# A depthwise convolution of 31 taps: for three of four channel chunks GpSimd sums eight of the taps

## The chip, the cores and the metric

The kernel runs on one core of a Trainium2 chip. The core's engines work side by side, each through its own queue in program order, and wait for each other at semaphores: TensorE (PE, matmuls; PEld its weight loads), VectorE (DVE), ScalarE (ACT), GpSimd (POOL), and SyncE (SP), which issues the DMAs. The metric is the time of one execution on the device in microseconds, less is better. Everything is in float32; a matmul in full precision is made of three passes over a high and a low part of its operands.

## What is computed

One decoder layer of 1024 tokens and 1024 channels. The part that the change touches is the causal convolution of group B: 512 channels, each with its own 31 taps along the sequence.

```python
def _conformer_conv(u, conv_w, conv_b, norm_g, norm_b):
    a, g = jnp.split(u, 2, axis=-1)
    glu = a * jax.nn.sigmoid(g)
    y = lax.conv_general_dilated(
        glu, conv_w[:, None, :], window_strides=(1,),
        padding=[(CONV_K - 1, 0)],
        feature_group_count=CONV_CH) + conv_b
    y = _layernorm(y, norm_g, norm_b)
    return jax.nn.silu(y)
...
proj = h @ w_in                       # q, k, v, index q/k/w, conv input
attn_out = _dsa_attention(q, k, v, qi, ki, wi)   # top 256 keys of a row
conv_out = _conformer_conv(cu, conv_w[i], conv_b[i], ...)
x = x + gt1 * (concat([attn_out, conv_out]) @ w_out)
u = square(relu(h2 @ w_up));  x = x + gt2 * (u @ w_down);  rmsnorm
```

## The kernel before, in words

The sequence is worked in two halves of 512 tokens (hf 0 and 1), with blocks of 128 tokens for attention (0 to 3 and 4 to 7). Each engine's queue has a fixed order. A scheduler makes it from the steps of the strings ORDER and TAIL and from a table of priorities PR, where a lower number is more urgent; the work of a step with a high number fills the gaps that the scheduler sees in its own estimate. The numbers that matter: loading weights ("feed") 32050; the convolution of the first half ("conv0") 998450 and of the second ("conv1") 401000; the projections to q 400000; the search passes 150050 and up; conv_norm and conv_out 190500 and 998500; the MLP 1000000.

Weights come in units (load_unit, from line 161): SP issues the DMA into one of two wraw buffers of two units each, ScalarE copies the unit to its high part whi (line 184), and GpSimd subtracts it from the unit to give the low part wlo (line 185), 128 x 512 numbers. The high and the low parts stand in a ring of WB = 3 tiles of two units, six units, so a unit's whi waits until TensorE has finished with the unit six before it. The projections to q and to the indexer's q run in mm3_pair (line 128, matmuls at line 137): for pairs of token blocks, over the 8 slices of the contraction, the passes high-high, high-low, low-high, so that every third matmul reads wlo. A q projection of half the blocks uses eight units: four for two pairs of blocks each, and then four others. Ahead of it stands the g projection (conv input and gate, 16 units, matmuls at line 126), which ends in glu.

The convolution (conv_chunk, line 634) works on a chunk j of 128 channels on the partitions and 512 tokens. A chunk's sum is built in the one PSUM tile cv. VectorE's tensor_scalar (line 641) makes tap 0 and adds the bias, then 30 scalar_tensor_tensor (line 643) multiply a shifted view of glu (SBUF) by the tap's weight cwT and add cv; the last writes y, in SBUF. With four chunks in each half these are 8 and 240 instructions. y of the first half uses the buffer "y0" that the sums of the modulation (adacc) used before; these are read last by the matmuls of line 537. conv_norm (BN at line 864, line 871) normalises over channels after a transpose on TensorE, conv_out (line 873) transposes back and applies SiLU on ScalarE.

Around it stand the searches for the 256th score of each row (line 660): for each of 31 bits ScalarE's Sign pass counts (line 680), and VectorE sets a flag and the next trial value (lines 682, 683), for two blocks in turn. A search thus has 62 flags. select (from line 686) makes the mask, attention and attention1 use it. The search "s3" (blocks 2 and 3) runs beside the first q projection, "s7" (blocks 6 and 7) beside the last convolution chunks, "s5" follows. out_proj(1) comes after the last attention; the first 11 groups of the first half's MLP (line 964 on) fill TensorE's gaps and must be done before it, since their weights come ahead of out_proj's in the ring.

Of the kernel before, what the change touches and what calls it, by code (L numbers as in the profile page):

```python
# [15 lines left out]
OP = mybir.AluOpType  # L16
# [10 lines left out]
CK = 31  # L27
# [17 lines left out]
RV = True  # L45
ORDER = "Q0 g0 i2 c q0 i3 s3 Q1 m S3 q1 a0 g1 a1 n0 a2 z0 a3 i6 i7 o i5 h i4 s7 s5"
WB = 3
FLAGP = False
START = "x0 x1 x2 x3 a0 p0 x4 x5 x6 x7 a1 p1 a2 p2 a3"
WORK = "a0 t0 t1 t2 t3 e0 h0 a1 e1 k0 h1 a2 e2 k1 r4 t4 t5 h2 a3 e3 k2 h3 k3 t6 t7"  # L50
# [22 lines left out]
def layer(ctx, tc, x, c, positions, w_ada, b_ada, g_mix, w_in, conv_w, conv_b,  # L73
          conv_norm_g, conv_norm_b, w_out, g_mlp, w_up, w_down, g_final, out, dump=None):
    nc = tc.nc
    V, A, P, T, SP = nc.vector, nc.scalar, nc.gpsimd, nc.tensor, nc.sync
# [4 lines left out]
    @contextmanager  # L81
    def prio(p):
        old = tc.cur_priority
        tc.cur_priority = p
        yield
        tc.cur_priority = old
# [17 lines left out]
    def cv_tile(n=512):  # L104
        return psum.tile([128, n], FT, name="cv", bufs=1)
# [33 lines left out]
    def split_w(raw, n, lo_engine=None):  # L139
        hi = wpool.tile([128, 1024], FR, name="whi", bufs=WB)  # L140
        lo = wpool.tile([128, 1024], FR, name="wlo", bufs=WB)
        with prio(PR["feed"]):
            A.activation(hi[:, :n], raw[:, :n], AF.Copy)
            (lo_engine or P).tensor_tensor(lo[:, :n], raw[:, :n], hi[:, :n].bitcast(FT), op=OP.subtract)
        return hi, lo
# [15 lines left out]
    def load_unit(src, nch, cols, gate=None, dst=None):  # L161
        if not ring:
            ring["raw"] = [wpool.tile([128, 1024], FT, name="wraw", bufs=2) for _ in range(2)]
            ring["hi"] = [wpool.tile([128, 1024], FR, name="whi", bufs=WB) for _ in range(WB)]
            ring["lo"] = [wpool.tile([128, 1024], FR, name="wlo", bufs=WB) for _ in range(WB)]
            ring["n"] = ring["m"] = 0
# [27 lines left out]
    cwT = const.tile([128, 4, CK], FT, name="cwT")  # L194
# [410 lines left out]
    ych, glus = {}, {}  # L605
# [28 lines left out]
    def conv_chunk(j, hf):  # L634
        tc.cur_priority = PR["conv1" if hf else "conv0"]
        if j == 0:
            ych[hf] = (ea if hf else ey).tile([128, 4, 512], FT, name="y", tag="ga" if hf else "y0", bufs=1)
        y = ych[hf][:, j, :]
        gl = glus[hf][:, j, :]
        s = cv_tile()  # L640
        V.tensor_scalar(s, gl[:, 0:512], cwT[:, j, 0:1], convb[:, j:j + 1], op0=OP.mult, op1=OP.add)
        for tap in range(1, CK):
            V.scalar_tensor_tensor(y if tap == CK - 1 else s, gl[:, tap:tap + 512], cwT[:, j, tap:tap + 1], s,  # L643
                                   op0=OP.mult, op1=OP.add)


    twice = const.tile([128, 64], FT, name="twice")
# [449 lines left out]
    for j in range(4):  # L1097
        conv_chunk(j, 1)
# [166 lines left out]
```

## Time and profile before

| | |
|---|---|
| median of 3 runs | 1375.25 us (1374.19 to 1385.54) |
| profiled execution | 1377.54 us, span 1375.8 us |
| TensorE busy | 1268.3 us, 92% |
| VectorE busy | 974.8 us, 71% |
| ScalarE busy | 683.5 us, 50% |
| GpSimd busy | 482.0 us, 35%, 396 instructions |

The span runs from the first to the last recorded instruction; the profiled execution's own time is 1.7 us longer. The chain is the sequence of work, each piece released by the one ahead of it, that ended last; only what shortens or lengthens it moves the time. "xN" counts instructions, "idle before, releaser" is how long the engine waited ahead of an instruction and for whom.

### The profile page before, as it was taken

What the parts mean: (1) busy time and instruction counts of PE and PEld (TensorE: products, weight loads), DVE (VectorE), ACT (ScalarE), POOL (GpSimd) and SP (SyncE); (2) the same over time, 40 slices, a digit from 0 to 9 for tenths busy, and PEclk for the clock granted to TensorE, in tenths of its full rate; (3) what the DMA queues carried; (4) which work ended last, traced back from release to release, by engine and by line L of the source; (5) the groups of instructions that cost most, each with busy time, mean ns of one, the idle gap of its engine ahead of it and who ended that gap; (6) DMA issues with size and microseconds to landing.
All of it is one profiled execution on the core that took longest, in us unless ns stands there. A gap on an engine that the chain in (4) does not pass through costs nothing.

```text
span 1375.8 us, 19421 instructions
## 1 busy us (share of the span) xinstructions
PE 1268.3 (92%) x6686; PEld 1065.7 (77%) x6686; DVE 974.8 (71%) x2074; ACT 683.5 (50%) x1376; POOL 482.0 (35%) x396
## 2 busy tenths in 40 slices
PE   4677899989998899989999999899999999999997
PEld 4676789978887678767887879777878877888875
DVE  4879889999898899997878762473443386343457
ACT  3323358855764888768983552333122223333332
POOL 1333434422144234452223216422222244444453
PEclk9688999999999899999999999999999999999999
DMA  9337735522143123222111122352111134323332
GB/s 319 121 115 224 226 79 155 139 62 70 31 139 110 60 70 93 92 70 61 62 47 54 62 77 85 130 192 83 47 45 49 54 107 162 93 91 101 94 98 91
DMA packets 135690, 139.55 MB, mean 101 GB/s; under 512 B 8877, under 2 KB 109833, under 8 KB 135592
## 3 DMA queue, kind: packets, MB, share of 16 engines
q1 hardware_dynamic: 135424, 138.22, 32.2%
q8 instruction: 52, 0.85, 0.3%
q14 instruction: 46, 0.38, 0.1%
q10 hardware_dynamic: 168, 0.11, 0.0%
HBM read 126.23 MB, written 12.06 MB: 101 GB/s over the span
## 4 chain that ended last, share of the span: by engine, by line
PE 68%; DVE 21%; DMA 4%; issue 3%; ACT 3%; POOL 1%; ACTq 0%; POOLq 0%; DVEq 0%; SPq 0%
PE mm L126 25%; PE mc L126 13%; PE mm L137 9%; PE tp L126 7%; DMA wa<-in_w_ada_dram 3%; PE po L841 2%; PE tp L834 2%; DVE acc L521 2%; DVE cv L643 1%; PE tp L309 1%; PE po L748 1%; PE mc L592 1%; DVE acc L1018 1%; PE mc L822 1%; DVE acc L316 1%
## 5 line engine op out<-in xcount | busy, mean ns | idle before, releaser
L185 POOL TENSOR_TENSOR wlo<-wraw,whi 128x512 fp32r<-128x512 f32 x310 | 416.7, 1352 | 754.2 <-ACT whi L184 698.0
L184 ACT ACTIVATE whi<-wraw 128x512 fp32r<-128x512 f32 x310 | 193.9, 629 | 292.1 <-PE mm L126 143.1
L126 PE MATMUL mm<-half,whi 128*128 128x512 f32 x608 | 207.4, 407 | 0.6 <-ACT half L957 0.6
L680 ACT ACTIVATE sj<-score,bits 128x512 uint8<-128x512 f32 (+5 forms) x186 | 163.2, 877 | 23.0 <-DVE bits L683 11.0
L643 DVE SCALAR_TENSOR_TENSOR cv<-glu,cwT,cv 128x512 f32<-128x512 f32 x232 | 174.0, 750 | 0.8
L126 PE MATMUL mm<-whi,uh 128*128 128x512 f32 x344 | 141.7, 412 | 14.3 <-DVE sq L979 8.2
L126 PE MATMUL mc<-half,whi 128*128 128x512 f32 x416 | 149.0, 390 | 0.1
L126 PE MATMUL mm<-whi,ul 128*128 128x512 f32 x344 | 138.8, 404 | 3.0 <-DVE ul L986 3.0
L126 PE MATMUL mm<-wlo,uh 128*128 128x512 f32 x344 | 139.4, 405 | 0.0
L984 DVE TENSOR_TENSOR sq<-sq 128x512 f32<-128x512 f32 x42 | 46.0, 1096 | 126.1 <-ACT sq L983 126.1
L1018 DVE TENSOR_TENSOR acc<-mm,acc 128x512 f32<-128x512 f32 x152 | 104.3, 687 | 39.8 <-PE mm L126 38.9
L126 PE MATMUL mc<-half,wlo 128*128 128x512 f32 x336 | 131.1, 390 | 0.0
L126 PEld LDWEIGHTS mm<-half,whi 128*128 128x128 f32 x608 | 114.2, 192 | 20.0 <-ACT half L957 0.8
L137 PE MATMUL mm<-whi,half 128*128 128x256 f32 x640 | 121.8, 286 | 3.2 <-DVE wi L450 3.0
L126 PE MATMUL mm<-half,wlo 128*128 128x512 f32 x304 | 123.1, 405 | 0.0
L137 PEld LDWEIGHTS mm<-whi,half 128*128 128x128 f32 x640 | 102.9, 194 | 5.7 <-issue 3.1
L126 PE MATMUL mc<-h,whi 128*128 128x512 f32 x256 | 99.9, 390 | 0.0
L126 PEld LDWEIGHTS mm<-whi,uh 128*128 128x128 f32 x344 | 66.5, 193 | 37.0 <-DVE sq L979 10.8
L137 PE MATMUL mm<-wlo,half 128*128 128x256 f32 x320 | 91.2, 285 | 0.0
L126 PEld LDWEIGHTS mc<-half,whi 128*128 128x128 f32 x416 | 78.0, 188 | 16.6 <-ACT half L957 0.5
L126 PEld LDWEIGHTS mm<-whi,ul 128*128 128x128 f32 x344 | 66.6, 194 | 18.7 <-DVE ul L986 4.3
L126 PEld LDWEIGHTS mm<-wlo,uh 128*128 128x128 f32 x344 | 66.8, 194 | 13.2
(312 smaller groups left out, 2657.4 us busy)
## 6 DMA issues: line engine op xcount, KB each, us to landing
wraw<-in_w_up_dram SPq DMA_DIRECT2D x108, 256.0 KB, 2.8
wraw<-in_w_down_dram SPq DMA_DIRECT2D x108, 256.0 KB, 2.8
wa<-in_w_ada_dram SPq DMA_DIRECT2D x48, 512.0 KB, 4.5
wraw<-in_w_in_dram SPq DMA_DIRECT2D x33, 256.0 KB, 2.8
wraw<-in_w_in_dram SPq DMA_DIRECT2D x64, 128.0 KB, 2.9
wraw<-in_w_out_dram SPq DMA_DIRECT2D x32, 256.0 KB, 2.7
xs<-in_x_dram SPq DMA_DIRECT2D x8, 512.0 KB, 4.5
x<-in_x_dram SPq DMA_DIRECT2D x8, 512.0 KB, 4.3
```

What stands on the lines that cost most here:

```text
L126: T.matmul(ps, x, y, start=first and i == 0, stop=last and i == 3 * n - 1)
L137: T.matmul(ps[:, i * 256:(i + 1) * 256], rows[i][k][x], w[k][y], start=m == 0, stop=m == len(steps) - 1)
L184: A.activation(hi, raw, AF.Copy)
L185: P.tensor_tensor(lo, raw, hi.bitcast(FT), op=OP.subtract)
L309: T.matmul(t[:, j, :], xs[b][:, k * 128:(k + 1) * 128], dg[b], start=True, stop=True)
L521: V.scalar_tensor_tensor(accs[s], w, cond[:, k:k + 1], accs[s], op0=OP.mult, op1=OP.add)
L643: V.scalar_tensor_tensor(y if tap == CK - 1 else s, gl[:, tap:tap + 512], cwT[:, j, tap:tap + 1], s, op0=OP.mult, op1=OP.add)
L680: A.activation(sj[:, :L], score[b], AF.Sign, bias=bits[:, col].bitcast(FT), accum_out=cnt[:, col])
L834: T.transpose(t[:, 2 * i + u, :], sbp[u][:, (i0 + i) * 128:(i0 + i + 1) * 128], ident)
L841: T.matmul(po[:, hp % 2], vhl[:, i0 + i, g].rearrange("p a d -> p (a d)"), p[:, 2 * i:2 * i + 2, :], start=i0 + i + j == 0, stop=i0 + i == ...
L984: V.tensor_tensor(sq, sq, sq, op=OP.mult)
L1018: V.tensor_tensor(acc[b][:, cols], ps, acc[b][:, cols], op=OP.add)
```

## The change

A new constant CP = 8. For the chunks 0, 1 and 2 of each half (chunk 3 stays as it was) GpSimd makes the taps 23 to 30: eight tensor_scalar, the first into y, the others into the place of the next chunk's y as scratch, and after each of those a tensor_tensor that adds the scratch to y. VectorE makes taps 0 to 22 in cv as before, and then adds cv and y to y with one tensor_tensor. In all GpSimd gets 48 multiplications and 42 additions, VectorE loses 48 scalar_tensor_tensor and gets 6 tensor_tensor.

```diff
+CP = 8
...
         y = ych[hf][:, j, :]
         gl = glus[hf][:, j, :]
+
+
+        nv = CK - CP if j < 3 else CK
+        for tap in range(nv, CK):
+            pr = y if tap == nv else ych[hf][:, j + 1, :]
+            P.tensor_scalar(pr, gl[:, tap:tap + 512], cwT[:, j, tap:tap + 1], None, op0=OP.mult)
+            if tap > nv:
+                P.tensor_tensor(y, pr, y, op=OP.add)
         s = cv_tile()
         V.tensor_scalar(s, gl[:, 0:512], cwT[:, j, 0:1], convb[:, j:j + 1], op0=OP.mult, op1=OP.add)
-        for tap in range(1, CK):
+        for tap in range(1, nv):
             V.scalar_tensor_tensor(y if tap == CK - 1 else s, gl[:, tap:tap + 512], cwT[:, j, tap:tap + 1], s,
                                    op0=OP.mult, op1=OP.add)
+        if nv < CK:
+            V.tensor_tensor(y, s, y, op=OP.add)
```

In the changed kernel all line numbers behind this function are 11 higher, those ahead of it 1 higher.

GpSimd's queue before, in the last part of the g projection ("x3" are three instructions that read alike; row 26 ends with the last unit but one of the g projection, row 28 is its last unit and the first two of the q projection, row 31 its units 3 to 6, and row 33 begins with units 7 and 8; score is the causal mask of a block, glu the copy of the taps' overlap):

```order
24 L185 TENSOR_TENSOR wlo<-wraw,whi 128x512 x6
25 L620 COPY glu<-glu 128x30
26 L185 TENSOR_TENSOR wlo<-wraw,whi 128x512 x3
27 L601 AFFINE_SELECT score_595<-score_595 128x128
28 L185 TENSOR_TENSOR wlo<-wraw,whi 128x512 x3
29 L620 COPY glu<-glu 128x30
30 L601 AFFINE_SELECT score_594<-score_594 128x128
31 L185 TENSOR_TENSOR wlo<-wraw,whi 128x512 x4
32 L620 COPY glu<-glu 128x30
33 L185 TENSOR_TENSOR wlo<-wraw,whi 128x512 x35
```

After, the same place. Line 186 is line 185 of before; lines 646 and 648 are the new multiplication and addition. Rows 28 and 33 are the last two units of the g projection; row 45, the next subtraction, is the first unit of the q projection.

```order
26 L186 TENSOR_TENSOR wlo<-wraw,whi 128x512 x2
27 L646 TENSOR_SCALAR y<-glu,cwT 128x512 x2
28 L186 TENSOR_TENSOR wlo<-wraw,whi 128x512
29 L602 AFFINE_SELECT score_595<-score_595 128x128
30 L646 TENSOR_SCALAR y<-glu,cwT 128x512
31 L648 TENSOR_TENSOR y<-y 128x512
32 L646 TENSOR_SCALAR y<-glu,cwT 128x512
33 L186 TENSOR_TENSOR wlo<-wraw,whi 128x512
34 L648 TENSOR_TENSOR y<-y 128x512
35 L646 TENSOR_SCALAR y<-glu,cwT 128x512
36 L648 TENSOR_TENSOR y<-y 128x512
```

Where subtractions and small operations stood alone, the first multiplications now stand ahead of the g projection's last two units. Further on in the same queue, from the sixth unit of the q projection (row 73) to its seventh and eighth, which are the first two of row 82:

```order
73 L186 TENSOR_TENSOR wlo<-wraw,whi 128x512
74 L648 TENSOR_TENSOR y<-y 128x512
75 L621 COPY glu<-glu 128x30
76 L646 TENSOR_SCALAR y<-glu,cwT 128x512
77 L648 TENSOR_TENSOR y<-y 128x512
78 L646 TENSOR_SCALAR y<-glu,cwT 128x512
79 L648 TENSOR_TENSOR y<-y 128x512
80 L646 TENSOR_SCALAR y<-glu,cwT 128x512
81 L648 TENSOR_TENSOR y<-y 128x512
82 L186 TENSOR_TENSOR wlo<-wraw,whi 128x512 x28
```

Of the first half's 24 multiplications and 21 additions 16 stand ahead of the q projection's first unit (row 45), 27 ahead of its third (row 59) and all 45 ahead of its seventh (row 82), where before there was nothing but other subtractions and four small operations; then 28 units follow without any of them. The second half's 45 stand in rows 83 to 128, 15 for each chunk, with runs of four units between the chunks and single ones inside the second and third.

VectorE's queue at the last tap of the second half, before (line 696 begins the selection after the search s7; line 775 prepares v for the last attention group):

```order
1027 L643 SCALAR_TENSOR_TENSOR y<-glu,cwT,cv 128x512
1028 L682 TENSOR_SCALAR flag<-cnt 128x1
1029 L683 TENSOR_SCALAR bits<-bits,flag 128x1
1030 L864 BN_STATS st_5235<-tp 128x6
1031 L865 BN_AGGR mv<-st_5235 128x2
1032 L682 TENSOR_SCALAR flag<-cnt 128x1
1033 L864 BN_STATS st_5235<-tp 128x6
1034 L979 TENSOR_SCALAR sq<-mm 128x512
1035 L683 TENSOR_SCALAR bits<-bits,flag 128x1
1036 L775 TENSOR_TENSOR vhl<-vv,vhl 128x16x64
1037 L682 TENSOR_SCALAR flag<-cnt 128x1
1038 L696 TENSOR_SCALAR thrs<-bits 128x1
```

And after, where line 652 is 643, 693 and 694 are 682 and 683, 875 is 864, and 1029 is 1018 (the MLP's sum):

```order
863 L652 SCALAR_TENSOR_TENSOR y<-glu,cwT,cv 128x512
864 L990 TENSOR_SCALAR sq<-mm 128x512
865 L694 TENSOR_SCALAR bits<-bits,flag 128x1
866 L693 TENSOR_SCALAR flag<-cnt 128x1
867 L875 BN_STATS st_5283<-tp 128x6
868 L1029 TENSOR_TENSOR acc<-mm,acc 128x512
869 L992 TENSOR_TENSOR sq<-sq 128x512
870 L1029 TENSOR_TENSOR acc<-mm,acc 128x512
871 L997 TENSOR_TENSOR ul<-sq,uh 128x512
872 L1029 TENSOR_TENSOR acc<-mm,acc 128x512
873 L694 TENSOR_SCALAR bits<-bits,flag 128x1
```

The last tap, which stood right ahead of the selection, now has 35 flags of the search between it and the selection (row 988), and the normalisation's rows lie among these. At the earlier steps (first flag of s3, its selection, the first attention, the end of the fourth) VectorE has the same number of convolution instructions behind it as before, within one or two, up to the middle of s7. TensorE's order is the same as before up to the middle of the second half's g projection. At the end of the last attention 72 matmuls of the first half's MLP are still to come in the order before, and 142 after.

## Rows read from the trace of the kernel before

**Rows 1.** The page: busy time by engine, and the chain that ended last.

```profile
PE 1268.3 (92%) x6686; PEld 1065.7 (77%) x6686; DVE 974.8 (71%) x2074; ACT 683.5 (50%) x1376; POOL 482.0 (35%) x396
...
PE 68%; DVE 21%; DMA 4%; issue 3%; ACT 3%; POOL 1%; ACTq 0%; POOLq 0%; DVEq 0%; SPq 0%
PE mm L126 25%; PE mc L126 13%; PE mm L137 9%; PE tp L126 7%; DMA wa<-in_w_ada_dram 3%; PE po L841 2%; PE tp L834 2%; DVE acc L521 2%; DVE cv L643 1%; PE tp L309 1%; PE po L748 1%; PE mc L592 1%; DVE acc L1018 1%; PE mc L822 1%; DVE acc L316 1%
```

**Rows 2.** Windows of 25 us: length, busy time (count) by engine, clock, DMA.

```profile
200.00:225.00 25.00, 25.00 (x210) 24.96 (x210) 24.15 (x70) 21.47 (x57) 11.64 (x11) 1.00 0.45 127
250.00:275.00 25.00, 25.00 (x187) 24.00 (x187) 24.14 (x79) 19.18 (x52) 11.29 (x9) 1.00 0.53 139
275.00:300.00 25.00, 21.13 (x117) 17.48 (x116) 23.73 (x62) 12.85 (x39) 7.46 (x6) 0.93 0.28 74
525.00:550.00 25.00, 25.00 (x113) 20.67 (x112) 24.13 (x59) 21.68 (x39) 11.61 (x9) 1.00 0.33 99
625.00:650.00 25.00, 25.00 (x132) 20.30 (x131) 17.60 (x50) 23.73 (x44) 7.27 (x6) 1.00 0.21 64
```

**Rows 3.** The chain of waits in order of time: start, us, piece.

```profile
175.28 1.50 PE po L537 x8
189.06 11.15 PE mm L126 x49
200.20 56.17 PE mm L137 x468
```

**Rows 4.** Timeline of GpSimd, 178 to 209 us: start, us, instruction, [idle before].

```profile
178.78 0.29 POOL L601 TENSOR_SCALAR_AFFINE_SELECT score<-score 128x128 f32<-128x128 f32 x1
...
187.52 1.30 POOL L185 TENSOR_TENSOR wlo<-wraw,whi 128x512 fp32r<-128x512 f32 x1 [4.73 <-ACT whi L184]
...
193.98 1.29 POOL L185 TENSOR_TENSOR wlo<-wraw,whi 128x512 fp32r<-128x512 f32 x1 [2.62 <-ACT whi L184]
195.69 1.29 POOL L185 TENSOR_TENSOR wlo<-wraw,whi 128x512 fp32r<-128x512 f32 x1 [0.41 <-ACT whi L184]
199.42 2.66 POOL L185 TENSOR_TENSOR wlo<-wraw,whi 128x512 fp32r<-128x512 f32 x2 [2.44 <-ACT whi L184]
...
208.27 4.10 POOL L185 TENSOR_TENSOR wlo<-wraw,whi 128x512 fp32r<-128x512 f32 x3 [6.04 <-ACT whi L184]
```

**Rows 5.** Single lines on VectorE: count, shortest/median/longest ns, first and last start.

```profile
L643 DVE SCALAR_TENSOR_TENSOR cv<-glu,cwT,cv x232: 705/750/757, 162.1 to 569.0; 128x512 f32<-128x512 f32 x116
L643 DVE SCALAR_TENSOR_TENSOR y<-glu,cwT,cv x8: 739/745/749, 209.3 to 569.8; 128x512 f32<-128x512 f32 x8
...
L521 DVE SCALAR_TENSOR_TENSOR acc<-wa,cond,acc x42: 734/747/1851, 91.1 to 172.3; 128x512 f32<-128x512 f32 x42
...
L683 DVE TENSOR_SCALAR bits<-bits,flag x186: 173/208/216, 196.3 to 724.0; 128x1 int32<-128x1 int32 x186
```

**Rows 6.** Groups by line and form: count, busy us, mean ns, idle before.

```profile
L1018 DVE TENSOR_TENSOR acc<-mm,acc 128x512 f32<-128x512 f32 x152 | 104.3, 687 | 39.8 <-PE mm L126 38.9
...
L495 DVE TENSOR_TENSOR qs<-qn,qs 128x512 fp32r<-128x512 f32 x14 | 13.2, 942 | 1.7 <-ACT qs L494 1.5
...
L601 POOL TENSOR_SCALAR_AFFINE_SELECT score<-score 128x128 f32<-128x128 f32 x6 | 1.9, 322 | 3.2 <-DVE score L599 3.2
...
L192 POOL MEMSET ones<- 128x128 f32 x1 | 0.2, 204 | 0.3 <-POOLq L1254 0.3
...
L1254 POOL MEMSET const-float32-0.0<- 128x1 f32 x1 | 0.1, 98 | 0.2 <-issue 0.2
```

**Rows 7.** Timeline of ScalarE, 207 to 220 us.

```profile
208.87 0.63 ACT L184 ACTIVATE whi<-wraw 128x512 fp32r<-128x512 f32 x1
...
219.00 0.63 ACT L184 ACTIVATE whi<-wraw 128x512 fp32r<-128x512 f32 x1 [0.24 <-issue]
```

**Rows 8.** Windows of line 643 alone: VectorE busy (count), clock, DMA.

```profile
525.00:550.00 25.00, 12.76 (x17) 1.00 0.33 99
550.00:575.00 25.00, 9.73 (x13) 1.00 0.32 96
```

## The prediction

> **What bounds the kernel now.** I read the page's busy line first, because it says which engine can't be the place to save. TensorE is busy in 92% of the span, VectorE in 71%, GpSimd in 35%, and the chain of work that ended last gives TensorE 68%, VectorE 21% and GpSimd 1%; the conv taps of line 643 hold 1% of it [rows 1]. So VectorE's 240 taps of 0.75 us, 180 us, are on the chain for some 14 us only: the reader should expect little from taking taps off VectorE, and ask what the change puts in front of TensorE.
>
> The windows say where. In 200 to 275 us TensorE is busy in all 25 us of each 25, at a granted clock of 1.00, VectorE in about 24, ScalarE in 19 to 21.5, and GpSimd in only 11 [rows 2]. The chain in order of time says what TensorE does there: the projections of line 137, 468 matmuls in 56.17 us, 0.12 us each, with nothing between them [rows 3]. They begin at 200.04 and have line 126's matmuls right ahead of them. In this stretch GpSimd makes wlo (line 185), the low half of each weight unit, and every third matmul reads one. The GpSimd timeline shows these subtractions at 1.3 us each, waiting for ScalarE's whi and hence early [rows 4]. GpSimd looks free there but is a supplier of the engine that sets the time.
>
> **How late wlo may be.** Call the eight units of the first query projection u1 to u8. A pair of row blocks takes 12 matmuls, 1.44 us, from each unit; u1 to u4 are used by two pairs in turn (11.5 us), then u5 to u8. TensorE's second matmul needs u1, so the needs are u1 200.15, u3 203.0, u4 204.5, u5 211.5, u6 213.0, u7 214.4, u8 215.8 us. In the timeline u3 and u4 start at 193.98 and 195.69, u5 and u6 at 199.42, u7 and u8 in the piece at 208.27 [rows 4]: 8, 8, 11 and, for u7, 5 us of slack with its 1.3.
>
> **What is removed.** Per half of the sequence VectorE loses 3 x 8 taps of 0.750 us and gains 3 adds with one PSUM and one SBUF operand, as line 1018 does in 0.687 [rows 5, 6]. In all 48 x 0.750 - 6 x 0.687 = 32 us of VectorE work go.
>
> **What is added.** GpSimd gets 48 multiplications by a per-channel number and 42 additions, all 128x512. An addition has the form of line 185: 1.30 us undisturbed [rows 4]. No row shows the multiplication. Bounds: filling 128x128 costs 106 ns more than filling 128x1 (204 against 98), hence 4 x 106 + 98 = 0.52 us at 512 for writing alone; the two-operand form, 1.3, is the top. Line 601's select, one operand in and one out, takes 0.32 (0.29 in the timeline) at 128 wide; less about 0.1 of start this is 0.19 per 128, 0.86 at 512 [rows 4, 6]. It is the nearest row, so I take 0.8. Each multiplication and addition of a chunk mostly waits for the one ahead of it; such a step costs between 0 and 0.2 us (no row shows it), and I take 0.13.
>
> The Trainium skill ("GPSIMD Engine Reference", 4.1, engine selection) advises against GpSimd for elementwise work on a tile, calling two-input operations about 2x slower and one-input ones roughly line rate; here 1.30 against VectorE's 0.69 agrees for two inputs. Line rate by that page's 1.2 GHz would be an estimated 0.43 us, and the same page (3.1) measures 769 ns for 512 elements of a tight loop. By the first the delay worked out below would be about 18 us, by the second 26.
>
> **Where it stands.** The order on GpSimd (the change section) puts the first two multiplications ahead of the last two subtractions of the g projection, and all of the first half's 24 multiplications and 21 additions ahead of u7. They can't start before about 176.6, since y shares its buffer with the sums that the eight matmuls of line 537 read last, at 175.28 for 1.50 [rows 3]. From there GpSimd has no idle time left:
> - up to u1: 9 multiplications, 7 additions, 2 subtractions, a select, gaps: 7.2 + 9.1 + 2.6 + 0.3 + 1.8 = 21.0, u1 ends 198.9, in time.
> - up to u3: 6, 5, u1 and u2, two small ones: its end is 215 against 203.0, 12 us late.
> - u4 218.4, late by 14 in all (the need moves with the delay); u5 227.7, by 16; u6 231.4, by 18.
> - u7: 24 x 0.8 + 21 x 1.3 + 8 x 1.3 + 1.0 + 45 x 0.13 = 63.8 after 176.6, so it starts at 240.4 instead of 208.3 and ends at 241.7 against 214.4: **27 us late**. u8 follows in time, and 28 subtractions come after it without a tap.
>
> With 0.52 and no gaps u7 ends at 229, 14 to 15 us late; with 1.3 and 0.2 at 257, 42 late.
>
> **Is the delay passed on?** TensorE has no idle time there to take it. ScalarE is in program order: its whi at 208.87 and 219.00 stand among the search's Sign passes [rows 7], and a whi needs a place in the ring of 6 units that TensorE gives back; the one at 219.00 needs u5's second pair, which moves by the 16 us of u5 and then by what u6 and u7 add to it, to about 246. Everything queued behind it on ScalarE waits: Sign passes of the search on blocks 2 and 3, hence VectorE's bits and the selection that attention starts from. So all engines move together. I give back 3 us, since ScalarE, 19 to 21.5 busy of 25, has some idle time there [rows 2], and add 2 for TensorE's clock: after the 4 us of idle time in 275 to 300 the granted clock is 0.93 [rows 2].
>
> **VectorE next to a busy GpSimd.** Line 643's taps, one operand in SBUF and one in PSUM, take 705 to 757 ns, GpSimd busy or not, and the search's bits 173 to 216; line 521, with two SBUF operands, 734 to 1851 [rows 5], the long ones beside a subtraction. The taps therefore stay at 0.75. Line 495's 14 operations have two as well and average 942 ns [rows 6]. The second half's 45 GpSimd operations lie beside some of these and of the rotations; at 0.2 us more each (942 less line 521's shortest, 734), thirty would cost 6, not all of it on the chain: I charge 3 (0 to 8, as some take 1 us more). The Trainium skill ("SBUF — State Buffer", on the shared port pair) says the same of these two kinds; the trace agrees, 750 against up to 1851.
>
> The new wait, VectorE's add for GpSimd's sum, stands in VectorE's queue ahead of search bits. Its three sums are ready at about 198, 221 and 240. The first add comes due 8 taps ahead of the last tap of before, which starts at 209.3 [rows 5], at about 203, the next ones some 21 us apart (22 taps, line 641 and the bits between them), at 225 and 246; so I cost it at nothing; a multiplication of 1.3 us would make it some 8 us late, but behind a larger delay of the same cause.
>
> **What comes back.** The freed VectorE time isn't taken as earlier ends: the order puts the same count of taps ahead of each step up to about 504 us, only from later chunks. The gain is there: 30 taps stand in 525 to 575 [rows 8], where VectorE is 24 of 25 busy [rows 2], and after the change the conv is done with 35 of the search's 62 flags still to come, so conv_norm and conv_out fit inside the search and the last attention group begins up to 25 us earlier. But TensorE's MLP of the first half, which fills the gaps of 575 to 832, must be done before out_proj of the second. In the order 70 of its matmuls (0.23 us apart, 16 us) move behind the last attention. The gain is 25 - 16 = 9 at best, less since ScalarE is 23.7 of 25 busy in 625 to 650 [rows 2]. I take 6 (0 to 16).
>
> **Sum**: 27 - 3 + 2 + 3 - 6 = +23 on the profiled execution's 1377.5 (span 1375.8), which is 2.3 above the median of 1375.25; against the median, **1398**.
>
> **Rivals.**
> 1. *Cheap multiplications and a full return, within 1%.* 0.52 and no gaps: 15 late, -3, +2, -10: about 1379. For it: filling is cheap [rows 6], VectorE is nearly full where it is relieved. Against: the select's price and the MLP still to be done.
> 2. *The other side: the tail of attention sets the end, faster.* If ScalarE and VectorE, not the MLP filler, decide when out_proj of the second half starts, the 25 us come through whole; with the 15 us delay and 3 of port trouble gone into ScalarE's idle time this is 1375 + 15 - 6 - 25 = 1359. It decides from a delay under 12 us or a return over 25. Against: TensorE is busy 25.0 of 25 in 625 to 650 [rows 2] with that filler.
> 3. *Multiplications as dear as additions, 42 late.* The second half's taps then also hold up the subtractions ahead of the first out_proj: 1375 + 42 + 3 = 1420. For it: the same engine needs 1.3 for the form it runs most [rows 4].
>
> **Chances.** Forecast 0.55, rival 3 0.20, rival 1 0.18, rival 2 0.07. One per cent, 14 us, is about what a measurement of this kernel can tell from no change. Slower by over 1% (above 1389) takes the forecast and rival 3, 0.75; within 1% 0.18; faster 0.07. The range 1378 to 1420 leaves out rival 2, the lower half of rival 1 and the worst of rival 3.
>
> **What would show it.** In the changed profile: GpSimd close to 25 of 25 busy from 177 to about 245, in place of 11; multiplications near 0.8 us; u7's subtraction near 240; TensorE idle before line 137, released by GpSimd's wlo, some 27 us in all, its block ending near 296 instead of 269; VectorE's taps still 750 ns; the second half's last tap well before the search ends. I am wrong if TensorE goes on at 204 without a wait, if u7 comes before 225, or if ScalarE's Sign passes end at 270 as before.

## The result, and the profile after

The changed kernel takes 1423.6 us (median of 4 runs, 1421.5 to 1426.6) against 1377.1 for the kernel before (4 runs by then): 1.0347 times as long, 95% interval 1.0307 to 1.0387 (the two medians alone give 1.0338), 46 us slower. The forecast was 1398 with a range to 1420: the right way, for the reason given, and half as much as came. The profiled execution has a span of 1420.7 us.

The page of the changed kernel, the lines of [rows 1]:

```profile
PE 1262.2 (89%) x6686; PEld 1064.2 (75%) x6686; DVE 952.1 (67%) x2032; ACT 682.6 (48%) x1376; POOL 609.3 (43%) x486
...
PE 66%; DVE 17%; POOL 8%; DMA 3%; issue 2%; ACT 2%; POOLq 0%; ACTq 0%; DVEq 0%; SPq 0%
PE mm L127 24%; PE mc L127 14%; PE mm L138 8%; PE tp L127 7%; POOL y L646 3%; DMA wa<-in_w_ada_dram 3%; POOL y L648 2%; PE po L852 2%; POOL wlo L186 2%; PE tp L845 2%; DVE acc L522 1%; PE tp L310 1%; PE po L759 1%; DVE acc L1029 1%; PE mc L593 1%
```

TensorE has as much to do as before but is busy in 89% of the span instead of 92%. VectorE lost 23 us of work (952 instead of 975), GpSimd gained 127 (609 instead of 482). GpSimd had 1% of the chain and now has 8%: its new lines 646 and 648 and the weights' low parts (now line 186) stand on it.

The windows of the two places where the time goes, 200 to 250 us and 375 to 400 us (columns as in [rows 2]; the first line is the kernel before, which [rows 2] leaves out, the others are the changed kernel):

```profile
225.00:250.00 25.00, 25.00 (x211) 25.00 (x210) 23.27 (x69) 21.64 (x59) 11.16 (x9) 1.00 0.56 159
...
200.00:225.00 25.00, 9.72 (x67) 9.72 (x68) 15.89 (x46) 11.14 (x29) 24.27 (x20) 0.62 0.14 37
225.00:250.00 25.00, 9.62 (x62) 8.92 (x61) 12.17 (x34) 8.97 (x24) 24.09 (x20) 0.79 0.12 32
...
375.00:400.00 25.00, 13.64 (x62) 11.49 (x63) 16.12 (x34) 7.01 (x17) 24.09 (x18) 0.73 0.14 43
```

Where TensorE had been busy in all 25 us at a clock of 1.00 it is busy in 10 at the first place, at a granted clock of 0.62 and 0.79 on average, and GpSimd, at 11 before, is busy in 24. The last rows of the first place on GpSimd (timeline, as [rows 4]):

```profile
244.66 1.56 POOL L646 TENSOR_SCALAR y<-glu,cwT 128x512 f32<-128x512 f32 x1
246.30 1.26 POOL L648 TENSOR_TENSOR y<-y 128x512 f32<-128x512 f32 x1
247.52 4.97 POOL L186 TENSOR_TENSOR wlo<-wraw,whi 128x512 fp32r<-128x512 f32 x4
```

The piece at 247.52 begins with the unit that the prediction calls u7, at 208.27 before; it expected 240.4. This execution reached line 537's end, where the taps can start, 7 us earlier than the kernel before, so the real shift is larger: 77.4 us after that end, not 31.5 as before and not the 63.6 of the prediction. The two new operations in the groups by form (busy us and mean ns behind the count):

```profile
L646 POOL TENSOR_SCALAR y<-glu,cwT 128x512 f32<-128x512 f32 x48 | 76.4, 1594 | 8.5 <-DVE glu L633 4.3 <-PE po L538 1.0
L648 POOL TENSOR_TENSOR y<-y 128x512 f32<-128x512 f32 x42 | 53.8, 1281 | 2.8
```

Who waited for whom between 190 and 260 us, on TensorE, on VectorE and on ScalarE (columns: total us, times, longest):

```profile
PE mm L138 <- ACT glu L632: 23.3, 1, 23.3
PE mm L138 <- POOL wlo L186: 15.4, 3, 9.8
...
DVE e L669 <- POOL score L602: 25.3, 1, 25.3
...
ACT sj L691 <- DVE bits L681: 25.9, 1, 25.9
```

The mask's row on GpSimd, before and after:

```profile
191.06 0.30 POOL L601 TENSOR_SCALAR_AFFINE_SELECT score<-score 128x128 f32<-128x128 f32 x1
...
208.34 0.29 POOL L602 TENSOR_SCALAR_AFFINE_SELECT score<-score 128x128 f32<-128x128 f32 x1
```

Here is something that the prediction did not name. VectorE first waits 25 us for the causal mask of a block (line 602, a select of 0.29 us on GpSimd that now stands behind taps). ScalarE's first Sign pass (line 691) waits for VectorE, the gate of the last glu chunk stands behind it in ScalarE's queue, and the query projection waits 23 us for that. Only then do the low parts hold it, 15 us more.

To compare stages, I count each profile from the end of line 537's last matmul (176.8 us before, 168 to 175 in the others: the loading ahead of it varies from execution to execution, also in e12, which differs from the kernel before only much later). The runs e1 to e16 are told in the next section; an out_proj starts here with the first of its sums on VectorE, and the end is that of the last DMA issue. What is later (+) or earlier than in the kernel before, in us:

| run | first q projection starts | ends | attention of block 3, last scores | first out_proj | last attention ends | second out_proj | end |
|---|---|---|---|---|---|---|---|
| before, from 537's end | 23.2 | 92.5 | 183.6 | 190.2 | 639.6 | 661.3 | 1195.8 |
| changed | +22 | +43 | +62 | +62 | +33 | +47 | +52 |
| e1, first half only | +22 | +44 | +47 | +43 | +25 | +41 | +42 |
| e2, second half only | -1 | -1 | +21 | +26 | +10 | +25 | +27 |
| e3, relief alone | +1 | +1 | +2 | +1 | -16 | 0 | +2 |
| e4, load alone | +22 | +43 | +66 | +70 | +73 | +73 | +75 |
| e6, four taps | +13 | +16 | +23 | +21 | +2 | +13 | +14 |
| e7, no power | +22 | +43 | +58 | +56 | +35 | +49 | +49 |
| e9, two operations | +11 | +23 | +34 | +34 | +8 | +23 | +23 |
| e10, four, two operations | +5 | +6 | +17 | +16 | -5 | +6 | +8 |
| e13, mask on VectorE | 0 | +42 | +73 | +67 | +50 | +64 | +67 |
| e14, e10 with the mask on VectorE | 0 | +1 | +13 | +8 | -2 | +13 | +16 |
| e16, relief with add | -1 | -1 | +3 | +2 | -26 | -12 | -8 |

In the changed kernel 43 us are lost up to the end of the first query projections (first place), 18 more up to the first out_proj (second place), 28 come back up to the end of attention, of which 14 are lost again ahead of the second out_proj, and 4 go behind it. Less the 7 us by which this execution loaded earlier, that is the 45 us between the two spans.

### The profile page after: what moved, and what is told of

It reads as the page before. It is cut to its first block, busy times and chain, and to the rows that moved or that the text cites. A ratio compares the mean times of both kernels' runs of the same rounds, so it can differ in the third digit from the quotient of the medians.

```text
span 1420.7 us, 19483 instructions
## 1 busy us (share of the span) xinstructions
PE 1262.2 (89%) x6686; PEld 1064.2 (75%) x6686; DVE 952.1 (67%) x2032; ACT 682.6 (48%) x1376; POOL 609.3 (43%) x486
## 3 DMA queue, kind: packets, MB, share of 16 engines
q1 hardware_dynamic: 135424, 138.22, 31.5%
## 4 chain that ended last, share of the span: by engine, by line
PE 66%; DVE 17%; POOL 8%; DMA 3%; issue 2%; ACT 2%; POOLq 0%; ACTq 0%; DVEq 0%; SPq 0%
PE mm L127 24%; PE mc L127 14%; PE mm L138 8%; PE tp L127 7%; POOL y L646 3%; DMA wa<-in_w_ada_dram 3%; POOL y L648 2%; PE po L852 2%; POOL wlo L186 2%; PE tp L845 2%; DVE acc L522 1%; PE tp L310 1%; PE po L759 1%; DVE acc L1029 1%; PE mc L593 1%
## 5 line engine op out<-in xcount | busy, mean ns | idle before, releaser
L138 PE MATMUL mm<-whi,half 128*128 128x256 f32 x640 | 125.7, 293 | 25.6 <-ACT glu L632 23.3
L652 DVE SCALAR_TENSOR_TENSOR cv<-glu,cwT,cv 128x512 f32<-128x512 f32 x190 | 142.4, 750 | 0.9
L127 PE MATMUL mm<-whi,uh 128*128 128x512 f32 x344 | 137.9, 401 | 4.0 <-DVE flag L693 2.0
L127 PE MATMUL mm<-wlo,uh 128*128 128x512 f32 x344 | 136.4, 396 | 0.0
L138 PEld LDWEIGHTS mm<-whi,half 128*128 128x128 f32 x640 | 106.2, 201 | 27.9 <-ACT glu L632 23.7
L138 PE MATMUL mm<-wlo,half 128*128 128x256 f32 x320 | 94.0, 294 | 15.4 <-POOL wlo L186 15.4
L646 POOL TENSOR_SCALAR y<-glu,cwT 128x512 f32<-128x512 f32 x48 | 76.4, 1594 | 8.5 <-DVE glu L633 4.3
```

The costliest lines, as they stand in the source:

```text
L127: T.matmul(ps, x, y, start=first and i == 0, stop=last and i == 3 * n - 1)
L138: T.matmul(ps[:, i * 256:(i + 1) * 256], rows[i][k][x], w[k][y], start=m == 0, stop=m == len(steps) - 1)
L646: P.tensor_scalar(pr, gl[:, tap:tap + 512], cwT[:, j, tap:tap + 1], None, op0=OP.mult)
```

## The experiments

The theory on which the first four were made (A): GpSimd's queue makes the weights' low parts late at two places, VectorE's relief gives some of it back. Rivals: the scheduler's other order costs the time (B), or GpSimd slows VectorE at the SBUF port (C). Each ratio below is to the kernel before, measured with the run, with its 95% interval; differences under 2% stand on these intervals alone.

**e1 and e2, one half each.**

```diff
-        nv = CK - CP if j < 3 else CK
+        nv = CK - CP if j < 3 and hf == 0 else CK      # e2: hf == 1
```

> GpSimd sums its eight taps in the first half of the sequence only; the second half is as before. Theory A (GpSimd's queue makes the weights' low parts late, in two places): the first place is unchanged, so the seventh unit of the first query projection still starts some 77 us after GpSimd's first multiplication, near 248, and the stage is some 43 us late; the second place, 375 to 400 us, is gone. With part of VectorE's relief back the time is 1405 to 1420. Theory B (the loss is one of order, the scheduler's other arrangement of VectorE's and TensorE's queues, not of GpSimd's time): no telling from the stage, the half with the change loses about half of the 46, about 1400. Theory C (VectorE is slowed by GpSimd at the SBUF port): taps longer than 0.76 us wherever GpSimd is busy.

> GpSimd sums its eight taps in the second half only; the first half is as before. Theory A: up to 280 us all as before (q projection block ends near 269); the 45 operations lie between the weight units of the first half's MLP and out_proj, which have some slack, so at most the 16 us of the second place are lost and the 13 to 30 us won in the last search and attention come back: 1362 to 1385. Theory B: about 1400. If each half's GpSimd work cost alike wherever it lies: 1400 too.

Measured: e1 1414.3 us, 1.0286 (1.0258 to 1.0313); e2 1402.2, 1.0203 (1.0169 to 1.0237). e1 is as theory A has it: the first place is whole, the second gone. e2 is a miss, 17 us above the range: the first place is untouched, but the second alone costs 26. What stops there shows in a window of the kernel before, the same of e2, and VectorE's waits in e2 and in the changed kernel:

```profile
325.00:350.00 25.00, 24.67 (x154) 20.91 (x153) 22.59 (x53) 16.93 (x36) 6.16 (x5) 1.00 0.18 55
...
325.00:350.00 25.00, 5.79 (x33) 5.03 (x32) 6.79 (x14) 2.76 (x8) 23.81 (x18) 0.64 0.04 10
...
DVE rs L211 <- POOL rs L210: 20.0, 1, 20.0
...
DVE rs L211 <- POOL rs L210: 11.5, 1, 11.5
```

In 325 to 350 all engines but GpSimd nearly stand still (TensorE, VectorE and ScalarE busy for 6, 7 and 3 us). VectorE waits 20 us for one 128x4 power of conv_norm (line 210 on GpSimd, 1 us), which is queued behind the second half's taps; the scores of the attention stand behind that wait in VectorE's queue, ScalarE's softmax behind them. In the changed kernel the same wait takes 11.5 us. What stops e2 at the second place is a small operation behind the taps, not weights: for a low part TensorE waits 3 us there.

**e3 and e4, relief alone and load alone.**

```diff
# e3: GpSimd's loop and the joining add are left out, VectorE's tap nv - 1 writes y
# e4: GpSimd's loop stays, VectorE makes all taps
-        for tap in range(1, nv):
+        for tap in range(1, CK):
...
-        if nv < CK:
-            V.tensor_tensor(y, s, y, op=OP.add)
```

> The taps 23 to 30 of three chunks are left out altogether (the result lacks them), so VectorE has the relief and GpSimd no new work. Theory A: no stage is late; the gain is what the changed kernel showed to come back behind the stages, 13 to 15 us at most, limited by the first half's MLP that must be done before the second out_proj: 1360 to 1375. If VectorE's 32 us were worth their whole length: 1345. Theory B: slower than before, since the order changes just as much.

> GpSimd does its 48 multiplications and 42 additions, VectorE still does all 31 taps and writes the result over GpSimd's sum. Theory A: the whole delay and no relief: 43 us at the first place, up to 16 at the second, 1425 to 1440, u7 near 248. Theory C: VectorE's taps next to GpSimd grow longer than 0.76 us and the time goes well beyond 1440. If GpSimd's work costs nothing by itself and the loss comes from VectorE's waits at its new add: near 1377.

Measured: e3 1375.4, 0.9998 (0.9972 to 1.0025); e4 1446.2, 1.0520 (1.0490 to 1.0551). GpSimd's work by itself costs 70 us, somewhat above the range; B falls as the cause of the loss (e3 has another order and loses nothing). C falls for the taps; line 652 of the changed kernel and of e4:

```profile
L652 DVE SCALAR_TENSOR_TENSOR cv<-glu,cwT,cv x190: 699/749/777, 158.1 to 557.1; 128x512 f32<-128x512 f32 x190
...
L652 DVE SCALAR_TENSOR_TENSOR cv<-glu,cwT,cv x232: 704/748/780, 160.7 to 635.5; 128x512 f32<-128x512 f32 x116
```

Their median is 749 and 748 ns, 750 before [rows 5], and the 69 and 62 of them that overlap one of GpSimd's new operations have the same medians. Whether C holds for other instructions of VectorE is taken up behind e14. And 36 us less work on VectorE are worth nothing in e3: attention ends 16 us earlier, but the chain of e3 shows what then fills TensorE:

```profile
800.66 10.14 PE mm L127 x43
...
810.83 7.12 PE mm L127 x30
...
822.40 8.01 PE mm L127 x34
830.41 5.86 PE mm L138 x48
```

These are the MLP's matmuls (line 127) that must be done before out_proj (line 138). They take the 16 us. In the kernel before, the chain holds this at the same point (line 126 is 127, line 137 is 138):

```profile
823.84 7.32 PE mm L126 x30
831.20 1.21 PE mm L126 x4
832.41 5.71 PE mm L137 x48
```

**e5, the price, and e8, a price list.** The multiplication had cost 1.59 us instead of the forecast's 0.8.

```diff
-            P.tensor_scalar(pr, gl[:, tap:tap + 512], cwT[:, j, tap:tap + 1], None, op0=OP.mult)
+            P.tensor_tensor(pr, gl[:, tap:tap + 512], cwT[:, j, tap:tap + 1].to_broadcast([128, 512]), op=OP.mult)
```

> The 48 multiplications on GpSimd are written as tensor_tensor with the tap's weight spread over the row, instead of tensor_scalar; all else is as in the changed kernel. Theory A1 (the dearer multiplication, 1.57 us instead of the 0.8 of the prediction, makes up what the stage is later than forecast): at the price of the two-operand form, 1.28, 24 of them give back 7 us at the first query projection and 2 to 4 at the second place, 1410 to 1417. Theory A2 (the price belongs to multiplying by a per-channel number, in whatever form): no change, 1424.

> A price list of one-operand forms on GpSimd, 128x512 where not said (the result is not the convolution): first half, chunk 0 multiplication by a constant, chunk 1 addition of the per-channel number, chunk 2 multiply and add; second half, chunk 0 multiplication by the per-channel number in two pieces of 256, chunk 1 a plain copy, chunk 2 the spread two-operand form. If the per-channel number is what costs, the constant and the copy take 0.8 or less; if it is the operation's own path, all tensor_scalar take about 1.57 and the copy less; two pieces of 256 take 0.85 each. The time is about that of the changed kernel, 1400 to 1440.

Measured: e5 1407.6, 1.0234 (1.0196 to 1.0273), 16 us better than the changed kernel, 2 us beyond what A1 allows. The form was cheaper than the expected 1.28:

```profile
L646 POOL TENSOR_TENSOR y<-glu,cwT 128x512 f32<-128x512 f32 x48 | 51.5, 1077 | 9.6 <-DVE glu L633 4.3 <-PE po L538 2.8
```

24 times the 0.52 us saved are 12, and the first place is 30 us late in e5 instead of 43. e8 took 1413.0 us in its one execution; its groups by form (line 649 a constant, 651 an addition of the channel's number, 653 multiply and add, 656 two pieces of 256, 658 a copy, 660 the spread two-operand form):

```profile
L656 POOL TENSOR_SCALAR y<-glu,cwT 128x256 f32<-128x256 f32 x16 | 15.5, 982 | 4.9 <-DVE glu L633 4.3
...
L651 POOL TENSOR_SCALAR y<-glu,cwT 128x512 f32<-128x512 f32 x8 | 12.5, 1568 | 0.3
L649 POOL TENSOR_SCALAR y<-glu 128x512 f32<-128x512 f32 x8 | 12.0, 1494 | 0.7
L660 POOL TENSOR_TENSOR y<-glu,cwT 128x512 f32<-128x512 f32 x8 | 8.9, 1112 | 0.5
L653 POOL TENSOR_SCALAR y<-glu,cwT 128x512 f32<-128x512 f32 x8 | 5.6, 697 | 0.6
...
L658 POOL COPY y<-glu 128x512 f32<-128x512 f32 x8 | 5.3, 671 | 0.4
```

Neither rule of the expectation holds. A constant is as dear as a channel's number (1.49 and 1.57 us), and doing more is cheaper: with a second operation the same instruction takes 0.70 us, little more than a copy (0.67). The second operation can be an addition of 0.0.

**e6, four taps.**

```diff
-CP = 8
+CP = 4
```

> GpSimd sums four taps instead of eight (CP = 4), VectorE one fewer than 28. Theory A: what counts is when GpSimd gets to each weight unit. In its queue all 12 multiplications and 9 additions stand ahead of the third unit of the first query projection, which then starts some 37 us after the first multiplication and is 12 to 13 us late, and nothing stands ahead of the seventh; with 0 to 5 us at the second place 1385 to 1393. Rival (a loss in proportion to GpSimd's work): half of 47, 1400. Rival (a loss that belongs to the second operand path, the add and its wait): 1424 less little.

Measured: 1386.6, 1.0087 (1.0057 to 1.0116), as A has it: half the taps cost a quarter of the loss, since GpSimd is done with them ahead of u3 and catches up before u7. The rivals (1400, 1424) fall. The one wait of TensorE at the first place is again the one behind the mask (12.3 us), not one for u3, which starts 37 us after the first multiplication as expected and would have held it about as long.

**e7, no power on GpSimd.**

```diff
-        P.tensor_tensor(dst, ms, half_c[:, :n], op=OP.pow)      # in conv_norm's rsqrt
+        V.tensor_scalar(dst, ms, 0.5, None, op0=OP.mult)
```

> The power in conv_norm's reciprocal root, one 128x4 operation on GpSimd, is replaced by a multiplication on VectorE (the norm's scale is then wrong); the eight taps stay. Theory A3 (the second place is VectorE's wait for that one power behind the second half's taps): the 11.5 us wait is gone, and with the stop of the other engines behind it 10 to 16 us come back, 1408 to 1414. Rival (the second place is late weight units, as at the first): 1424, with TensorE idle for a low part instead.

Measured: 1424.7, 1.0373 (1.0317 to 1.0430): nothing. That is the rival's number, but not for its reason, as TensorE waits only 2 us for a low part there. The wait is gone, and the first out_proj comes 5 us earlier than in the changed kernel; the second comes no earlier. In its place TensorE waits elsewhere:

```profile
PE tp L504 <- DVE qs L499: 11.2, 3, 5.6
```

So A3 is half right: the power holds the engines in e2 and in the changed kernel, but it isn't the only thing at the second place. e10, in which VectorE waits 0.7 us for the power, as in the kernel before, still loses 9 there.

**e9 and e10, the cheap form, with eight and with four taps.**

```diff
-            P.tensor_scalar(pr, gl[:, tap:tap + 512], cwT[:, j, tap:tap + 1], None, op0=OP.mult)
+            P.tensor_scalar(pr, gl[:, tap:tap + 512], cwT[:, j, tap:tap + 1], 0.0, op0=OP.mult, op1=OP.add)
```

> The changed kernel with one thing different: GpSimd's tensor_scalar is written with two operations, multiply by the weight and add the constant 0.0, the form that the price list showed at 0.70 us instead of 1.57; its queue has the same order. Theory A: 24 multiplications give back 24 x 0.87 = 21 us at the first query projection (seventh unit near 227 instead of 247.5, the stage 22 us late instead of 43), and the wait at the second place is gone, which the run without the power showed to be worth nothing at the end: 1397 to 1405. If the second place's 16 us counts too: 1385 to 1390. Rival (GpSimd's two-operation form is cheap only beside other forms, or slows the additions behind it): above 1410.

> Four taps, in the cheap form. Theory A: the third unit's lateness of the run with four taps, about 12 us, shrinks by 12 x 0.87 = 10 to some 2 us, so no stage is late by more than that, and VectorE's relief is worth nothing, as in the run with relief alone: 1371 to 1380. If relief does count once GpSimd isn't late: 1360 to 1366.

Measured: e9 1394.7, 1.0145 (1.0112 to 1.0179); e10 1380.8, 1.0036 (1.0018 to 1.0054). e9 is a little below its range, e10 a little above. With nothing changed but a second operation in an instruction, which adds 0.0, 29 of the 46 us are gone. The multiplication and u7 in e9:

```profile
L646 POOL TENSOR_SCALAR y<-glu,cwT 128x512 f32<-128x512 f32 x48 | 35.0, 733 | 8.4 <-DVE glu L633 4.3 <-PE po L538 0.9
...
224.95 4.99 POOL L186 TENSOR_TENSOR wlo<-wraw,whi 128x512 fp32r<-128x512 f32 x4
```

u7 starts 22.6 us earlier than in the changed kernel, 20.7 if counted from line 537's end, and 24 x (1.594 - 0.733) is 20.7; the first place is 23 us late instead of 43, as expected. The second place shrank from 18 to 11 (the table below says of what). e10 has 6 us at the first place instead of the expected 2.

**e11 and e12, ten groups of the MLP ahead of the second out_proj** (relief alone, and the kernel before).

```diff
-G0 = 11
+G0 = 10
...
-TAIL = "S7 m n z a7 a6 S5 a5 a4 f11 e o f0 h"
+TAIL = "S7 m n z a7 a6 S5 a5 a4 f10 e o f0 h"
```

> Relief alone (taps left out, as before), and the first half's MLP has 10 instead of 11 groups ahead of the second out_proj; the eleventh is done later with the rest. Theory D (VectorE's relief is worth nothing since TensorE has the same work and the same gaps; that the filler must be done is only where it shows): out_proj's second part starts some 15 us earlier than with relief alone, and the end is as it was, 1368 to 1380. Theory E (the filler ahead of out_proj holds back a gain that exists): 1355 to 1362.

> The kernel before with 10 groups ahead of the second out_proj, the counterpart of the run above without relief. Theory D: out_proj's second part starts 10 to 16 us earlier, the end within 8 us of before, 1368 to 1382. Theory E: nothing is gained without relief, 1376, and the difference to the run above is 15 us or more.

Measured: e11 1370.5, 0.9961 (0.9941 to 0.9980); e12 1382.1, 1.0045 (1.0025 to 1.0065). out_proj's second part starts 26 and 14 us earlier than with 11 groups; behind it e11 loses most of that (6 us are left at the end) and e12 more than all of it (its end is 8 us later), as D has it. But between the two lie 12 us: with ten groups the relief is worth 0.8%, with eleven nothing. Neither theory is whole.

**e13 and e14, the mask on VectorE**, with eight taps as changed and with four in the cheap form.

```diff
-        P.affine_select(d, d, pattern=[[-1, 128]], compare_op=OP.is_ge, fill=NEG, base=0, channel_multiplier=1)
+        V.tensor_tensor(d, d, caus[:, 128:256], op=OP.add)
```

> The changed kernel, but the causal mask of a block's scores (one 128x128 select on GpSimd, 0.29 us, which in the changed kernel stands behind the taps and for which VectorE waits 25 us at 208) is an addition on VectorE. Theory A (the weights decide): the first query projection starts at its old time, near 193 to 200, and then waits for its units one by one; the seventh still starts near 247, so the stage ends as late as in the changed kernel, 1412 to 1424. Theory F (what holds all engines is the mask, and the weights only follow): the wait of 23 to 25 us is gone for good, near 1400.

> Four taps in the cheap form (1381 so far, the query projection waiting 4.5 us behind the mask and no more for weights), and the mask on VectorE. If the small operation behind the taps was all of that 4.5 to 6.5 us: 1374 to 1378. If the third weight unit takes its place (it starts near 197 against a need near 196 to 197): 1379 to 1381.

Measured: e13 1438.4, 1.0453 (1.0423 to 1.0484); e14 1386.5, 1.0080 (1.0053 to 1.0107). e13 settles the first place. TensorE's waits there, and u7 (the piece at 250.93):

```profile
PE mm L138 <- POOL wlo L186: 33.2, 7, 10.1
...
250.93 4.96 POOL L186 TENSOR_TENSOR wlo<-wraw,whi 128x512 fp32r<-128x512 f32 x4
```

The projection starts on time and ends 42 us late, as in the changed kernel: it waits for its units seven times. The mask only held what the units would have held. That e13 is slower still, 14 us above the range, comes from the second place (25 us instead of 18, with 18.9 us of waiting for the power instead of 11.5) and from what comes back up to the end of attention (17 us instead of 28, why is open). In e14 the first place costs 1 us, as hoped for, but its time is worse than e10's: attention ends 3 us later by the table, and the second out_proj starts 8 later. The expectations of both runs missed.

The second place, taken apart. For each run the table has how much longer than before the stretch from the end of the first q projections to the first out_proj is, how long VectorE waits in it for the power, and how much longer VectorE's instructions in it take in sum than the same lines in the kernel before (us):

| run | stretch | wait for the power | instructions longer |
|---|---|---|---|
| before | 0 | 0.7 | 0 |
| changed | 18.6 | 11.5 | 6.9 |
| e2, second half only | 26.6 | 20.0 | 4.4 |
| e13, mask on VectorE | 25.0 | 18.9 | 5.1 |
| e7, no power | 13.1 | none | 9.5 |
| e9, two operations | 10.7 | 1.9 | 8.2 |
| e10, four, two operations | 9.3 | 0.7 | 5.8 |
| e6, four taps | 5.4 | 0.7 | 4.0 |
| e16, no taps on GpSimd | 3.0 | 0.7 | -0.1 |

The two together are the loss but for 1 to 4 us, and e16's order alone makes 3. The instructions that grow are not the taps but mostly those with two operands in SBUF, such as the rotations (line 457 of the kernel before, 2.1 us in the changed kernel) and in some runs the low parts of line 888, and the scaling of line 871. So rival C holds for these. Over the whole span e16 and the changed kernel give VectorE the same number of instructions, 2032, and beside GpSimd's taps they keep it busy 9 us longer (952.1 in the changed kernel's page above; here is e16's):

```profile
PE 1260.6 (93%) x6686; PEld 1063.5 (78%) x6686; DVE 943.0 (69%) x2032; ACT 683.6 (50%) x1376; POOL 482.7 (35%) x396
```

This is a sum from the traces; no run takes the longer instructions away by themselves.

**e15, the parts together** (e14 with ten groups), and **e16, relief with the add kept** (e3, but VectorE joins an unweighted row of glu).

```diff
# e16, against the changed kernel: GpSimd's loop is left out, and
-            V.tensor_tensor(y, s, y, op=OP.add)
+            V.tensor_tensor(y, s, gl[:, nv:nv + 512], op=OP.add)
```

> The run above with 10 groups of the first half's MLP ahead of the second out_proj, which with VectorE's relief alone was worth 5 us: 1369 to 1376, the best that these parts add up to, and no measurable gain on the kernel before. If the relief comes through further once nothing is late: 1360 to 1366.

> As relief alone (taps left out), but VectorE keeps the joining add, here of an unweighted row of glu, so that its queue holds what it holds in the changed kernel, with no work on GpSimd. In the runs with both parts 10 to 14 us came back between the two out_proj, in relief alone 1. If that comes from the scheduler's order, which the add changes: 1362 to 1368. If it comes from time that TensorE loses to GpSimd earlier, in which other work gets done: 1373 to 1378.

Measured: e15 1383.0, 1.0042 (1.0020 to 1.0064), a miss, and no version that makes all taps beats the kernel before. e16 1362.2, 0.9917 (0.9881 to 0.9952): with six more additions than e3, and in the order that the scheduler makes of them, the relief is worth 14 us. Attention ends 26 us earlier instead of 16, and the MLP then takes 14 of it. That is what came back in the changed kernel too (28, of which 14 were lost again). Why e3's order keeps 10 us of it is open; by the count of the table the last flag of the last search comes 7 us earlier than before in e3 and 13 in e16, and the first scores of the last attention group 22 and 32.

## Why the prediction was right and wrong

- **What bounds the kernel, and where the change strikes**: right for the larger place. TensorE waits at the first query projection for what GpSimd makes, ScalarE and VectorE move along: the search s3 ended 44 us later than before by the count of the table, the projection 43.
- **"So I take 0.8"**: this step failed. The multiplication takes 1.57 us, above even the upper bound of 1.3, which rested on the idea that an instruction with one operand can't cost more than one with two; the select of [rows 6] from which 0.8 was taken is no guide to this form, only to the one with two operations (0.70). The rule of the Trainium skill that the prediction weighed ("GPSIMD Engine Reference", 4.1, one-input operations at roughly line rate) doesn't hold for it either: 1.57 us, where the prediction's estimate of line rate is 0.43. The waits between dependent operations, on the other hand, cost next to nothing: 45 of them and all small gaps took 2 us, not 6. Together u7 was done 78.7 us after line 537's end instead of 65, and the stage was 43 us late instead of 27. e5 and e9, in which only the price differs, show it: 12 and 20 us of those 43 go with 0.5 and 0.86 us per multiplication (24 of them).
- **That u7 is the unit that decides**: right, and e13 shows it against the mask, which the prediction had only counted as a small operation in the queue. What the prediction missed is that all engines waited for that mask first.
- **"The second half's taps": charged 3 us at the SBUF port, and in a rival at the first out_proj's weights.** This term failed too: the second place cost 18. The prediction had costed GpSimd's queue for large operations and overlooked the power in it, for which VectorE and all behind it wait (11.5 us; 20 in e2). Without the power (e7) the place still costs 13, so the wait isn't all of it: VectorE's instructions were 6.9 us longer there in the changed kernel, the effect of [rows 5] with more than twice the 3 us taken, inside the stated 0 to 8. The two add up to the 18.
- **VectorE's taps stay at 0.75 us; the add waits for nothing that matters**: right, by the taps' rows of e4 and the changed kernel; ahead of the six adds (line 655) VectorE stood idle for 0.3 us in all.
- **"The gain is 25 - 16 = 9 at best", 6 taken**: the mechanism was right, the size not. 28 us came back between the first out_proj and the end of attention, and the MLP's matmuls took 14 of them; e16 shows 14 us with no taps on GpSimd at all. This is also the most that was seen to come of the relief: 1% of the time, for 32 us less on VectorE.
- **Sum**: forecast 27 - 3 + 2 + 3 - 6 = 23; measured 43 + 18 - 14 + 4 = 51 by the count of the table, 46 between the medians. The 3 us that ScalarE was to give back weren't seen. The 2 for the clock are inside the 43: the first query projections took 21 us longer, 15.4 of them waits, and the rest, up to 6, passes with the lowered clock. No run bears on the 4 behind the second out_proj.
- **The rivals**: the third, multiplications as dear as additions, was nearest. It gave 1420 and its chance was 0.20; the multiplications were dearer than that. That its number came so near is partly luck: it has nothing come back, and holds the first out_proj by weights.

## What to carry to other kernels

An engine with 35% of busy time isn't free if what it makes is read at once by the engine that sets the time: go through its queue and ask, for every operation behind the added block, the small ones first (a mask, a power), who waits for it and how long it may be late. Ask too which instructions of VectorE run beside the block: here the taps kept their time, many of those with two operands in SBUF didn't. A price that no row shows should be measured in a kernel of a few lines before it is bounded by "simpler can't be dearer", and an instruction's forms belong to that list. And work taken off a busy engine is worth what the order behind it makes of it: here 0 us for 36 and, in another order, 14 for 32.

## What the runs showed of the hardware

GpSimd's tensor_scalar on 128x512 float32 takes 1.57 us with one operation and a per-channel number, 1.49 with one and a constant, and 0.70 with two operations, multiply and add 0.0; two pieces of 256 with one operation take 0.98 each, a copy 0.67, the two-operand form 1.28, and 1.08 to 1.11 where one operand is spread over the row. Beside such work VectorE's taps, with one operand in SBUF, kept their 0.75 us, while its 2032 instructions together took 9 us longer than in e16. While TensorE stood waiting for 15 of each 25 us at the first place, its granted clock fell from 1.00 (the level of 2.4 GHz) to 0.50 (the level of 1.2 GHz) in 200 to 213 us and again in 245 to 250, on average to 0.62 in 200 to 225 and 0.79 in 225 to 250, and the projection's matmuls then took 0.15 us each for a while instead of the 0.12 of [rows 3]:

```profile
248.84 11.16 PE mm L138 x75
```
